# The last out-projection: token tiles in pairs, seven quarter products in place of eight

## The chip, the core and the metric

The kernel runs on one core of one Trainium2 chip. The metric is the device time of one execution in microseconds (us), the median over several runs. A core has TensorE (PE, matmuls; PEld is its loading of weights), VectorE (DVE), ScalarE (ACT), GpSimd (POOL) and SyncE (SP, which here only issues DMAs). Engines run their own queues in order and wait for each other by semaphores.

## The reference

A trunk of two layers over 2064 tokens (16 meta tokens and 2048 tokens) of 1024 channels. Layer 0 is a gated convolution module, layer 1 gated linear attention (GLA). After each layer comes a residual sum and a LayerNorm:

```python
for i in range(DEPTH):                       # DEPTH = 2
    if i % N_MIXERS == 0:
        y = conformer_mixer(h, ...)
    else:
        y = gla_mixer(h, ...)                # ends with (o * silu(r)) @ w_out
    h = layer_norm(DN_ALPHA * h + y, post_ln_g[i], post_ln_b[i])
return h[:, N_META:]
```

What the change touches is the end of layer 1 alone: `(o * silu(r)) @ w_out`, a product of 2048 x 1024 by 1024 x 1024, the sum with `DN_ALPHA * h`, the LayerNorm and the store of the output. All is float32.

## The kernel before

Four phases follow each other: the convolution layer's projections and taps (`phase1`), its norm, gate and out-projection (`phase2`), the GLA projections and chunks (`phase3`), and the last out-projection (`phase4`). A float32 product is made of three matmuls: each operand is split into a high part (a copy on ACT in the reduced type) and a low part (a subtraction on VectorE or GpSimd; `split`, L72 to 74), and `mm3` (L102 to 108) adds high times high, high times low and low times high into one PSUM bank, for each of eight blocks of 128 channels.

`phase4` (L825 to 869) first drives `phase3` to its end; the generator `gla` holds the last steps of the last head. Then the loop over 16 tiles of 128 tokens: `gated` loads a tile of gated outputs from `og_d` (L836) and splits it; `xt` gets the residual (L857); `out_tile` (L372 to 377) runs 24 matmuls for each half of 512 columns and adds the PSUM bank to `xt` (row sum, L377); `ln_stats` (L379 to 389) takes mean and variance with two instructions on VectorE, an aggregate, and a power on GpSimd (L388); four scale-and-shift instructions on VectorE (L862, L864) finish the tile, which is stored (L868; the last one in two halves, L866).

PSUM for these products is three banks in turn (`pjt`). The splits use three pairs of buffers in turn (`pair`). The weights of the out-projection stand in SBUF in high and low parts, loaded and split by `load_half` (L810 to 822) while the last heads run. The small tiles of `phase4` (`rowb`, `xt`) reuse tags of phase 3's pool `hp` (opened in `phase3_init`, L464), so they take over single buffers of it.

The program is written with a tile framework: it traces the instructions in the order of the code and, when the program is built, sets the order on every engine by a list scheduling over a simulated timeline (`schedule_with_timeline_sim=True`); of the instructions that are ready, that which stands earlier in the code goes first. So the splits of a later tile can lie between steps of an earlier one. A tile that takes over memory of a closed pool waits for the last use of what lay there (`reuse_waits="tile"`).

## Time and profile before

| what | value |
|---|---|
| median of 3 runs | 1761.71 us (1760.18 to 1763.15) |
| profiled execution, its own time | 1762.52 us |
| its span, first to last instruction | 1760.8 us |
| TensorE busy | 1703.8 us, 97% |
| VectorE busy | 1401.8 us, 80% |
| GpSimd busy | 940.5 us, 53% |
| ACT busy | 844.8 us, 48% |
| matmuls in the last out-projection | 768 |

Busy time is the sum of the instructions' own times. Matmuls overlap in a pipeline, so their listed duration is longer than the distance from one to the next; the distance of starts is what a matmul costs in a full stream. Times in the views are counted from the span's start. A view of an engine in order of time gives start, duration, the instruction and, in brackets, the idle time before it and what ended that. The profiled execution is one run; its own time, and not the median, is what its spans add up to.

### The profile page before, as it was taken

To read this page: it belongs to the slowest core of one execution; us is meant where nothing else is said; L and a number is where in the kernel's file an instruction comes from. 1 tells how busy PE (TensorE), PEld (TensorE's weight loads), DVE (VectorE), ACT (ScalarE), POOL (GpSimd) and SP (SyncE) were. 2 spreads that over 40 slices of the span, in tenths; PEclk is the share of its full clock that TensorE was granted. 3 is DMA by queue.
4 is the path that set the end of the run, shared out by engine and by line. 5 is a ranking of instruction groups with operands and counts; after the bars stand their busy time and mean duration, and the time that the engine had idled before them with its cause. 6 is when DMAs were issued, how large, how long until landed. Compare 5 with 4: busy or idle time off the path is not lost.

```text
span 1760.8 us, 29085 instructions
## 1 busy us (share of the span) xinstructions
PE 1703.8 (97%) x11715; PEld 1515.1 (86%) x11715; DVE 1401.8 (80%) x1893; ACT 844.8 (48%) x1293; POOL 940.5 (53%) x675
## 2 busy tenths in 40 slices
...
DMA packets 103911, 178.72 MB, mean 102 GB/s; under 512 B 8624, under 2 KB 68400, under 8 KB 103776
## 3 DMA queue, kind: packets, MB, share of 16 engines
...
q14 instruction: 43, 0.35, 0.1%
...
## 4 chain that ended last, share of the span: by engine, by line
PE 67%; DVE 17%; ACT 5%; POOL 4%; issue 4%; DMA 2%; SPq 0%; DVEq 0%; POOLq 0%; ACTq 0%
PE pj_y L107 4%; PE pj_y L108 4%; PE pj_y L106 4%; PE pj_g L107 3%; PE pj_g L106 3%; PE pj_g L108 3%; PE pj_z L107 3%; PE pj_a L107 3%; PE pj_z L106 3%; PE pj_a L106 3%; PE pj_z L108 3%; PE pj_a L108 3%; DVE A L712 2%; DVE A L711 2%; PE att L718 1%
## 5 line engine op out<-in xcount | busy, mean ns | idle before, releaser
L196 POOL TENSOR_TENSOR gacc<-gacc,prod 128x1024 f32<-128x1024 f32 (+1 forms) x156 | 386.3, 2479 | 64.6 <-ACT prod L195 55.7
L204 DVE SCALAR_TENSOR_TENSOR cacc<-glu,prm,cacc 128x1024 f32<-128x1024 f32 (+1 forms) x292 | 374.9, 1294 | 7.0
L708 POOL TENSOR_TENSOR A<-b 128x256 f32<-128x256 f32 x96 | 79.6, 829 | 305.1 <-PE att L718 119.1
L195 ACT ACTIVATE prod<-glu,prm 128x1024 f32<-128x1024 f32 (+1 forms) x156 | 179.3, 1156 | 108.4 <-POOL gacc L196 108.0
L106 PE MATMUL pj_g<-xh,h_w 128*128 128x412 f32 (+1 forms) x320 | 114.1, 357 | 6.0 <-ACT h_w L73 4.3
L107 PE MATMUL pj_g<-xl,h_w 128*128 128x412 f32 (+1 forms) x320 | 114.0, 356 | 0.3 <-DVE xl L74 0.3
L108 PE MATMUL pj_y<-woh,l_gt 128*128 128x512 f32 (+1 forms) x272 | 108.6, 405 | 5.2 <-DVE l_gt L74 5.1
L108 PE MATMUL pj_g<-xh,l_w 128*128 128x412 f32 (+1 forms) x320 | 112.7, 353 | 0.0
L107 PE MATMUL pj_a<-xl,h_w 128*128 128x412 f32 (+1 forms) x320 | 112.4, 351 | 0.0
L106 PE MATMUL pj_a<-xh,h_w 128*128 128x412 f32 (+1 forms) x320 | 112.3, 351 | 0.0
L107 PE MATMUL pj_z<-xl,h_w 128*128 128x412 f32 (+1 forms) x320 | 112.3, 351 | 0.0
L106 PE MATMUL pj_z<-xh,h_w 128*128 128x412 f32 (+1 forms) x320 | 112.2, 351 | 0.0
L108 PE MATMUL pj_z<-xh,l_w 128*128 128x412 f32 (+1 forms) x320 | 112.0, 351 | 0.0
L108 PE MATMUL pj_a<-xh,l_w 128*128 128x412 f32 (+1 forms) x320 | 111.9, 350 | 0.0
L106 PE MATMUL pj_y<-woh,h_gt 128*128 128x512 f32 (+1 forms) x272 | 110.4, 409 | 0.8 <-ACT h_gt L73 0.6
L107 PE MATMUL pj_y<-wol,h_gt 128*128 128x512 f32 (+1 forms) x272 | 110.3, 406 | 0.0
L106 PE MATMUL pj_y<-w4h,h_g 128*128 128x512 f32 x256 | 99.7, 390 | 0.0
L107 PE MATMUL pj_y<-w4l,h_g 128*128 128x512 f32 x256 | 99.6, 390 | 0.0
L108 PE MATMUL pj_y<-w4h,l_g 128*128 128x512 f32 x256 | 99.5, 389 | 0.0
L645 ACT ACTIVATE A<-A 128x512 f32<-128x512 f32 (+1 forms) x112 | 66.8, 598 | 55.1 <-POOL A L709 54.4
L388 POOL TENSOR_TENSOR rs<-rs,mhalf 128x1 f32<-128x1 f32 x16 | 14.5, 907 | 145.8 <-DVE rs L387 145.8
L377 DVE SCALAR_TENSOR_TENSOR xt<-xt,pj_y 128x512 f32<-128x512 f32 (+1 forms) x66 | 44.5, 678 | 59.2 <-PE pj_y L108 59.1
...
## 6 DMA issues: line engine op xcount, KB each, us to landing
r_w<-w SPq DMA_DIRECT2D x24, 512.0 KB, 3.2
c<-c_d SPq DMA_DIRECT2D x16, 512.0 KB, 4.6
szb<-sz_d SPq DMA_DIRECT2D x16, 512.0 KB, 4.5
xt<-x_tok SPq DMA_DIRECT2D x16, 512.0 KB, 4.6
h_d<-xt SPq DMA_DIRECT2D x16, 512.0 KB, 2.8
r_h1b<-h_d SPq DMA_DIRECT2D x16, 512.0 KB, 3.9
...
xt<-h_d SPq DMA_DIRECT2D x16, 512.0 KB, 3.5
```

The lines of the kernel that those rows point to most:

```text
L106: mm(out, lhsT=lh, rhs=rh, start=(i == 0), stop=False)
L107: mm(out, lhsT=lh, rhs=rl, start=False, stop=False)
L108: mm(out, lhsT=ll, rhs=rh, start=False, stop=(i == n - 1))
L195: nc.scalar.activation(pr, src(k), AF.Copy, scale=tap(k))
L196: nc.gpsimd.tensor_tensor(st["g"], st["g"], pr, op=ALU.add)
L204: nc.vector.scalar_tensor_tensor(out, src(k), tap(k), acc, op0=ALU.mult, op1=ALU.add)
L377: self.nc.vector.scalar_tensor_tensor(xt[:m, es], xt[:m, es], ALPHA, ps, op0=ALU.mult, op1=ALU.add)
L645: ex = lambda o, i: nc.scalar.activation(o, i, AF.Exp, scale=1.0 / TAU)
L708: nc.gpsimd.tensor_tensor(Av[:, :, 0], mid, bv[:, :, 0], op=ALU.subtract)
L711: nc.vector.tensor_tensor(Av[:, :, 0], Av[:, :, 0], kv[:, :, 0], op=ALU.mult)
L712: nc.vector.tensor_tensor(Av[:, :, 1], Av[:, :, 1], qv[:, :, 1], op=ALU.mult)
L718: nc.tensor.matmul(att[s : s + m, c, s + m : s + 2 * m], lhsT=A[:, a : a + m], rhs=A[:, a + m : a + 2 * m], start=False, stop=False, skip_ ...
```

## The change

Tiles 0 to 3 are computed as before. Tiles 4 to 15 go in six pairs. A pair is a block of 2 by 2 quarters: two tiles by two halves of the 1024 channels; the weight is 2 by 2 quarters as well. The pair's product is made of seven products of quarters (each 12 matmuls of 512 columns: four blocks of 128 channels, three matmuls each) in place of eight. For this,

- four sums of quarters of each pair are formed ahead (`forms`: two on VectorE, two on GpSimd) and split, with the two quarters of the first tile and one of the second;
- four sums of quarters of the weight are formed once (`weight_sums`, four calls during tiles 0 to 2, in the order 0, 3, 1, 2), from a second load of the weight, with subtractions on GpSimd and VectorE, and split;
- the products accumulate in three PSUM banks `x`, `y`, `z`: a bank is read after one product and the next product adds onto it (`add=True` in `mm3`). The first product goes through ACT to `s1` and is added to three of four quarters of the residual by GpSimd; the others are added by VectorE (`row_sum`, `add`);
- mean and variance of tiles 0 to 13 are taken by two passes on ACT with an accumulator; the last pair keeps `ln_stats`.

Residual tiles now hold a pair (two buffers), row vectors are whole rows, and all tiles of the phase lie in a new pool `p4`, opened after phase 3's pools `hp`, `c` and `gp` are closed. `weight_sums` stages its loads in the two buffers `junk`, which the ACT passes also use for their output.

```diff
--- before.py
+++ after.py
@@ -99,11 +99,11 @@
             out += [(h[:, k], l[:, k]) for k in range(nk)]
         return out
 
-    def mm3(self, out, ops):
-
-        mm, n = self.nc.tensor.matmul, len(ops)
+    def mm3(self, out, ops, add=False):
+
+        mm, n = partial(self.nc.tensor.matmul, skip_group_check=add), len(ops)
         for i, (lh, ll, rh, rl) in enumerate(ops):
-            mm(out, lhsT=lh, rhs=rh, start=(i == 0), stop=False)
+            mm(out, lhsT=lh, rhs=rh, start=(i == 0 and not add), stop=False)
             mm(out, lhsT=lh, rhs=rl, start=False, stop=False)
             mm(out, lhsT=ll, rhs=rh, start=False, stop=(i == n - 1))
 
@@ -461,8 +461,9 @@
         self.a1x = [c0.tile([P, P], F32, name=f"a1x{i}") for i in range(2)]
         for t in self.a1x:
             nc.gpsimd.memset(t, 0.0)
-        self.hp = self.pool(self.st3, name="p3h", bufs=2)
-        c = self.pool(self.st3, name="p3c", bufs=1)
+        self.st3l = ExitStack()
+        self.hp = self.pool(self.st3l, name="p3h", bufs=2)
+        c = self.pool(self.st3l, name="p3c", bufs=1)
         self.prm = c.tile([P, 8], F32, name="prm3")
         nc.sync.dma_start(self.prm[:, 0:6], pp)
         nc.vector.tensor_scalar(self.prm[:, 6:8], self.prm[:, 4:6], 0.5, None, op0=ALU.mult)
@@ -474,7 +475,7 @@
         nc.vector.tensor_tensor(self.wa2[64:96], raw[64:96], self.wa2[64:96], op=ALU.subtract)
         with ExitStack() as st:
             self.gla_consts(c, self.pool(st, name="p3k", bufs=1))
-        self.gp = self.pool(self.st3, name="p3g", bufs=2)
+        self.gp = self.pool(self.st3l, name="p3g", bufs=2)
         self.S = {}
 
     def block(self, bi):
@@ -819,12 +820,14 @@
             nc.sync.dma_start(r, wo[4 * e + k])
             self.split(r, h[:, k], l[:, k], nc.gpsimd if k == 1 else nc.vector)
             self.w4.append((h[:, k], l[:, k]))
+        self.w4t.append((h, l))
 
 
 
     def phase4(self, wo, rows, out):
         nc = self.nc
-        self.w4 = []
+        self.w4, self.w4t = [], []
+        self.uid = iter(range(1 << 20))
         gla = self.phase3(wo)
 
         last = (self.slot - 1) % len(self.slots)
@@ -845,27 +848,140 @@
             pass
         for _ in gla:
             pass
-        rb = []
-        for r, tags in enumerate((("gl", "ah"), "kq")):
-            rb.append([self.hp.tile([P, BMAX], F32, tag=t, name=f"rowb{r}{t}", bufs=1 + r)[:, :512] for t in tags])
+        self.st3l.close()
+        p4 = self.pool(self.st3, name="p4", bufs=1)
+        rb = [p4.tile([P, D], F32, name=f"rowb{r}") for r in range(2)]
+        for r in range(2):
+            nc.sync.dma_start(rb[r], rows[r : r + 1].broadcast_to([P, D]))
+        pairt = lambda nm, bufs=1: p4.tile([P, 2, D], F32, tag=nm, name=f"{nm}4_{next(self.uid)}", bufs=bufs)
+        half = lambda e: slice(512 * e, 512 * (e + 1))
+        last_pair = len(SUBS) // 2 - 1
+        add, sub = (partial(nc.vector.tensor_tensor, op=o) for o in (ALU.add, ALU.subtract))
+        gadd, gsub = (partial(nc.gpsimd.tensor_tensor, op=o) for o in (ALU.add, ALU.subtract))
+
+        def residual(p):
+            xt = pairt("xt", 2)
+            o = NMETA + 2 * P * p
+            nc.sync.dma_start(xt, self.h1_d[o : o + 2 * P].rearrange("(t p) d -> p t d", p=P))
+            return xt
+
+        def row_sum(ps, x):
+            nc.vector.scalar_tensor_tensor(x, x, ALPHA, ps, op0=ALU.mult, op1=ALU.add)
+
+        def norm_out(p, t, xt):
+            x, nm = xt[:, t], f"4{p}_{t}"
+            tk = slice(P * (2 * p + t), P * (2 * p + t + 1))
+            if p == last_pair:
+                rs = self.ln_stats(p4, x, P, nm)
+                mean, sub_mean = rs[:, 0:1], ALU.subtract
+            else:
+                rs = p4.tile([P, 4], F32, tag="rs4", name=f"rs{nm}", bufs=4)
+                junk = p4.tile([P, D], F32, tag="junk", name=f"junk{nm}", bufs=2)
+                nc.scalar.activation(junk, x, AF.Identity, accum_out=rs[:, 3:4])
+                nc.vector.tensor_scalar(rs[:, 0:1], rs[:, 3:4], -1.0 / D, None, op0=ALU.mult)
+                nc.scalar.activation(junk, x, AF.Square, bias=rs[:, 0:1], accum_out=rs[:, 1:2])
+                nc.vector.tensor_scalar(rs[:, 1:2], rs[:, 1:2], 1.0 / D, LN_EPS, op0=ALU.mult, op1=ALU.add)
+                nc.gpsimd.tensor_tensor(rs[:, 2:3], rs[:, 1:2], self.mhalf[:, 0:1], op=ALU.pow)
+                mean, sub_mean = rs[:, 0:1], ALU.add
             for e in range(2):
-                nc.sync.dma_start(rb[r][e], rows[r : r + 1, 512 * e : 512 * (e + 1)].broadcast_to([P, 512]))
-        for i in range(16):
-            tk = slice(P * i, P * (i + 1))
+                nc.vector.scalar_tensor_tensor(x[:, half(e)], x[:, half(e)], mean, rb[0][:, half(e)], op0=sub_mean, op1=ALU.mult)
+            for e in range(2):
+                nc.vector.scalar_tensor_tensor(x[:, half(e)], x[:, half(e)], rs[:, 2:3], rb[1][:, half(e)], op0=ALU.mult, op1=ALU.add)
+                if p == last_pair:
+                    nc.sync.dma_start(out[tk, half(e)], x[:, half(e)])
+            if p < last_pair:
+                nc.sync.dma_start(out[tk], x)
+
+
+
+        f12 = [p4.tile([P, 2, 4, 512], F32R, name=f"f12{x}") for x in "hl"]
+        f3 = [p4.tile([P, 4, 512], F32R, name=f"f3{x}") for x in "hl"]
+        f4 = [t[:, :, 512:] for t in self.w4t[0]]
+        w11, w21, w22 = ([x[:, :, half(e)] for x in self.w4t[k]] for k, e in ((0, 0), (1, 0), (1, 1)))
+        t4 = None
+
+        def weight_sums(k):
+            r1, r2 = (p4.tile([P, D], F32, tag="junk", name=f"ws{k}_{i}", bufs=2) for i in range(2))
+            nc.sync.dma_start(r1, wo[k])
+            nc.sync.dma_start(r2, wo[4 + k])
+            t12, t3 = (p4.tile([P, 2, 512], F32, tag=f"s{i}", name=f"t{i}_{k}") for i in (12, 34))
+            gsub(t12[:, 0], r1[:, half(1)], r1[:, half(0)])
+            sub(t3[:, 0], r2[:, half(1)], r1[:, half(1)])
+            gsub(t12[:, 1], r2[:, half(1)], t12[:, 0])
+            gsub(t4[k // 2][:, k % 2], r2[:, half(0)], t12[:, 1])
+            self.split(t12, f12[0][:, :, k], f12[1][:, :, k], nc.vector)
+            self.split(t3[:, 0], f3[0][:, k], f3[1][:, k], nc.vector)
+
+
+        t4 = [p4.tile([P, D], F32, tag=f"c{i}", name=f"t4{i}").rearrange("p (k c) -> p k c", k=2) for i in range(2)]
+        for i in range(4):
+            p, t = divmod(i, 2)
+            xt = xt if t else residual(p)
             h, l = gated(i, self.raw(f"c4{i}")[:, :D]) if i else g0
-            xt = self.hp.tile([P, 4, 256], F32, tag="vh" if i % 2 else "vl", name=f"xt4{i}").rearrange("p a b -> p (a b)")
-            nc.sync.dma_start(xt, self.h1_d[NMETA + P * i : NMETA + P * (i + 1)])
-            self.out_tile(h, l, self.w4, xt, P, f"y4{i}")
-            rs = self.ln_stats(self.gp, xt, P, f"4{i}")
-            halves = [slice(512 * e, 512 * (e + 1)) for e in range(2)]
-            for e, es in enumerate(halves):
-                nc.vector.scalar_tensor_tensor(xt[:, es], xt[:, es], rs[:, 0:1], rb[0][e], op0=ALU.subtract, op1=ALU.mult)
-            for e, es in enumerate(halves):
-                nc.vector.scalar_tensor_tensor(xt[:, es], xt[:, es], rs[:, 2:3], rb[1][e], op0=ALU.mult, op1=ALU.add)
-                if i == 15:
-                    nc.sync.dma_start(out[tk, es], xt[:, es])
-            if i < 15:
-                nc.sync.dma_start(out[tk], xt)
+            for e in range(2):
+                ps = self.pjt(f"y4{i}_{e}")
+                self.mm3(ps, [(h[:, k], l[:, k], self.w4[k][0][:, half(e)], self.w4[k][1][:, half(e)]) for k in range(KD)])
+                row_sum(ps, xt[:, t, half(e)])
+            if i < 3:
+                weight_sums(i)
+                if not i:
+                    weight_sums(3)
+            norm_out(p, t, xt)
+        for i in range(2):
+            self.split(t4[i], *(x[:, 2 * i : 2 * i + 2] for x in f4), nc.vector)
+
+        def forms(p):
+
+            c = []
+            for t in range(2):
+                r = self.raw(f"c4{p}_{t}")[:, :D] if p % 2 == 0 else p4.tile([P, D], F32, tag=f"c{t}", name=f"c4{p}_{t}")
+                o = P * (2 * p + t)
+                nc.sync.dma_start(r.rearrange("p (k n) -> p k n", n=P), self.og_d[:, :, o : o + P])
+                c.append(r.rearrange("p (a n) -> p a n", a=2))
+            (a11, a12), (a21, a22) = ((x[:, 0], x[:, 1]) for x in c)
+            s12, s34 = (p4.tile([P, 2, 512], F32, tag=f"s{i}", name=f"s{i}_{p}") for i in (12, 34))
+            two = lambda nm: [t[:, :D].rearrange("p (a n) -> p a n", a=2) for t in self.pair(nm)]
+            a1 = two(f"g4a{p}")
+            self.split(c[0], *a1, nc.vector)
+            add(s12[:, 0], a21, a22)
+            sub(s12[:, 1], s12[:, 0], a11)
+            b = two(f"g4b{p}")
+            self.split(s12, *b, nc.vector)
+            gsub(s34[:, 0], a11, a21)
+            gsub(s34[:, 1], a12, s12[:, 1])
+            d = two(f"g4c{p}")
+            self.split(s34, *d, nc.vector)
+            e = [p4.tile([P, 1, 512], F32R, tag=f"a22{x}", name=f"a22{x}_{p}") for x in "hl"]
+            self.split(a22, *(x[:, 0] for x in e), nc.vector)
+            q = lambda pr, i: [x[:, i].rearrange("p (k n) -> p k n", n=P) for x in pr]
+            return q(a1, 0), q(b, 1), q(a1, 1), q(d, 0), q(b, 0), q(e, 0), q(d, 1)
+
+        for p in range(2, last_pair + 1):
+            xt = residual(p)
+            fs = forms(p)
+            x, y, z = (self.pjt(f"y4{p}_{i}") for i in range(3))
+            prod = lambda ps, f, w, add: self.mm3(ps, [(f[0][:, k], f[1][:, k], w[0][:, k], w[1][:, k]) for k in range(4)], add)
+            f1, f2 = ([t[:, i] for t in f12] for i in range(2))
+            prod(x, fs[0], w11, False)
+            s1 = p4.tile([P, 512], F32, tag="p1", name=f"p1_{p}")
+            nc.scalar.activation(s1, x, AF.Copy, scale=1.0 / ALPHA)
+            gadd(xt[:, 0, half(1)], xt[:, 0, half(1)], s1)
+            x1 = xt[:, 1].rearrange("p (e c) -> p e c", e=2)
+            gadd(x1, x1, s1.unsqueeze(1).to_broadcast([P, 2, 512]))
+            prod(y, fs[1], f2, False)
+            row_sum(y, xt[:, 0, half(1)])
+            prod(x, fs[2], w21, True)
+            row_sum(x, xt[:, 0, half(0)])
+            prod(y, fs[3], f3, True)
+            row_sum(y, xt[:, 1, half(1)])
+            prod(z, fs[4], f1, False)
+            add(xt[:, 1, half(1)], xt[:, 1, half(1)], z)
+            prod(y, fs[5], f4, True)
+            row_sum(y, xt[:, 1, half(0)])
+            prod(z, fs[6], w22, True)
+            add(xt[:, 0, half(1)], xt[:, 0, half(1)], z)
+            norm_out(p, 1, xt)
+            norm_out(p, 0, xt)
         self.st3.close()
 
 
```

## Rows read from the trace of the kernel before

**Rows 1.** The busy table of the page: busy us, share of span, x instructions.

```profile
PE 1703.8 (97%) x11715; PEld 1515.1 (86%) x11715; DVE 1401.8 (80%) x1893; ACT 844.8 (48%) x1293; POOL 940.5 (53%) x675
```

**Rows 2.** Busy time by stage: length, busy by engine, granted clock, DMA share, GB/s.

```profile
core 0: us, PE busy (x) PEld busy (x) DVE busy (x) ACT busy (x) POOL busy (x), PEclk, DMA share, GB/s
...
1680.00:1700.00 20.00, 20.00 (x90) 16.57 (x89) 11.78 (x19) 2.13 (x2) 0.92 (x1) 1.00 0.47 155
...
1740.00:1761.00 21.00, 11.96 (x53) 9.57 (x51) 10.17 (x18) 0.00 (x0) 1.83 (x2) 0.87 0.13 51
```

**Rows 3.** Groups by line, 1400 to 1761: busy us, mean ns, idle before.

```profile
L106 PE MATMUL pj_y<-w4h,h_g 128*128 128x512 f32 x256 | 99.7, 390 | 0.0
```

**Rows 4.** VectorE in order of time, tiles 5 and 6: start, duration, instruction.

```profile
1643.20 0.69 DVE L377 SCALAR_TENSOR_TENSOR xt<-xt,pj_y 128x512 f32<-128x512 f32 x1 [4.02 <-PE pj_y L108]
1643.92 0.69 DVE L385 BATCH_NORM_STATS2 st<-xt 128x6 f32<-128x512 f32 x1
1644.53 1.21 DVE L74 TENSOR_TENSOR l_g<-r_c,h_g 128x1024 fp32r<-128x1024 f32 x1
1645.66 0.20 DVE L386 BATCH_NORM_AGGREGATE rs<-st 128x2 f32<-128x12 f32 x1
1645.89 0.15 DVE L387 TENSOR_SCALAR rs<-rs 128x1 f32<-128x1 f32 x1
...
1646.62 0.75 DVE L862 SCALAR_TENSOR_TENSOR xt<-xt,rs,rowb0ah 128x512 f32<-128x512 f32 x1
1647.29 0.75 DVE L864 SCALAR_TENSOR_TENSOR xt<-xt,rs,rowb1k 128x512 f32<-128x512 f32 x1
...
1654.08 0.69 DVE L377 SCALAR_TENSOR_TENSOR xt<-xt,pj_y 128x512 f32<-128x512 f32 x1 [4.02 <-PE pj_y L108]
```

**Rows 5.** Groups by line on ACT, 1540 to 1752.

```profile
L73 ACT ACTIVATE h_g<-r_c 128x1024 fp32r<-128x1024 f32 x15 | 15.9, 1063 | 115.0 <-PE pj_y L107 106.5 <-DMA r_c<-og_d 4.5 <-issue 4.0
...
L769 ACT ACTIVATION_READ_ACCUMULATOR kh<-o 128x1 f32 x8 | 1.6, 196 | 0.0
```

**Rows 6.** Groups by line and shape on GpSimd, whole span.

```profile
L423 POOL TENSOR_TENSOR xt<-xt,row 128x1024 f32<-128x1024 f32 x16 | 42.4, 2651 | 9.9 <-DVE xt L377 9.2 <-DVE rsl L331 0.7
...
L74 POOL TENSOR_TENSOR a_l<-at,a_h 128x512 fp32r<-128x512 f32 x16 | 24.5, 1534 | 81.7 <-ACT a_h L73 81.7
```

**Rows 7.** GpSimd in order of time, 1567 to 1575.

```profile
1567.93 0.61 POOL L708 TENSOR_TENSOR A<-b 128x256 f32<-128x256 f32 x1 [9.21 <-PE att L718]
...
1571.47 3.38 POOL L74 TENSOR_TENSOR w4l<-r_w,w4h 128x1024 fp32r<-128x1024 f32 x1
```

**Rows 8.** One line's instructions: duration ns min/median/max, first and last start.

```profile
L711 DVE TENSOR_TENSOR A<-A,b3k x24: 401/427/2618, 1411.6 to 1576.9; 128x256 f32<-128x256 f32 x24
```

**Rows 9.** VectorE in order of time, 1570 to 1576.

```profile
1570.96 1.63 DVE L74 TENSOR_TENSOR w4l<-w,w4h 128x1024 fp32r<-128x1024 f32 x1
1572.52 2.62 DVE L711 TENSOR_TENSOR A<-A,b3k 128x256 f32<-128x256 f32 x1
```

**Rows 10.** One line's instructions in the first stage (columns as in rows 8).

```profile
L204 DVE SCALAR_TENSOR_TENSOR cacc<-glu,prm,cacc x292: 1273/1290/1309, 57.5 to 541.1; 128x1024 f32<-128x1024 f32 x76, 128x1040 f32<-128x1040 f32 x70
L204 DVE SCALAR_TENSOR_TENSOR cacc<-glu,prm,gacc x16: 1301/3420/3512, 53.6 to 510.3; 128x1024 f32<-128x1024 f32 x8, 128x1040 f32<-128x1040 f32 x8
```

**Rows 11.** TensorE in order of time, the last transposes of phase 3.

```profile
1611.74 1.03 PE L780 MATMUL oT<-ident,osb 128*128 128x128 f32 x8
```

**Rows 12.** VectorE in order of time, 1614 to 1622.

```profile
1614.53 0.75 DVE L782 SCALAR_TENSOR_TENSOR og<-oT,prm,b3r 128x512 f32<-128x512 f32 x1
...
1621.44 0.69 DVE L377 SCALAR_TENSOR_TENSOR xt<-xt,pj_y 128x512 f32<-128x512 f32 x1 [3.51 <-PE pj_y L108]
```

**Rows 13.** DMA issues, 1540 to 1761: count, KB each, median us to landing.

```profile
w<-wo SPq DMA_DIRECT2D x2, 512.0 KB, 3.4
```

**Rows 14.** VectorE in order of time, the end of the kernel.

```profile
1752.00 0.69 DVE L377 SCALAR_TENSOR_TENSOR xt<-xt,pj_y 128x512 f32<-128x512 f32 x1 [4.02 <-PE pj_y L108]
...
1755.75 0.74 DVE L864 SCALAR_TENSOR_TENSOR xt<-xt,rs,rowb1q 128x512 f32<-128x512 f32 x1
```

## The prediction

> **What bounds the kernel now.** I read the busy table, then the table by stage of the end, then one tile of the last out-projection on VectorE. TensorE is busy for 97% of the span [rows 1]. In the last stage it never stops: 20.00 us of every 20 us up to 1740, at full clock, with VectorE near 11.8 us and GpSimd under 2 us [rows 2]. The stage is 16 tiles of 48 matmuls, 768 in three groups of 256 [rows 3]. Their listed 0.39 us is the length of one in a pipeline, not its price. The price comes from the row sums of the same half of two successive tiles, at 1643.20 and 1654.08: 10.88 us for 48 matmuls, 0.2267 us each [rows 4]. VectorE waits 4.02 us there for TensorE, so TensorE sets the pace. The order on each engine is fixed when the program is built, so an instruction that is late holds back all behind it on its engine.
>
> **What is removed.** A pair of tiles takes 96 matmuls, eight products of 12; seven take 84. Six pairs save 72 x 0.2267 = 16.3 us. All of it is TensorE time in a stage where TensorE is the bound, so it is the whole possible gain, 0.93%. A pair would take 84 x 0.2267 = 19.04 us, a product 2.72. The statistics on VectorE (two of 0.69 us, one of 0.20 and one of 0.15 a tile [rows 4]) leave it in 14 tiles; VectorE idles there now, so this gives nothing by itself.
>
> **VectorE and ACT in a pair.** By the distance of starts in [rows 4] a split of 1024 columns costs 1.13 us on VectorE, a scale-and-shift instruction of 512 columns 0.665, a row sum out of PSUM about 0.69. An add of 512 columns I estimate as half a split, 0.6. A pair has 3.5 splits (4.0), two adds (1.2), six reads of PSUM (4.1), eight scale-and-shift (5.3) and small ones (0.6): 15.2 us of the 19.04. ACT gets 3.5 copies of 1.06, one of 0.6, and four passes for the statistics of about 1.06 + 0.19 [rows 5]: near 9.5 us. Both fit. Loads and stores are the same bytes for the tiles; the DMA share stays near its 0.47 [rows 2].
>
> **GpSimd and VectorE take turns.** A pair adds on GpSimd three adds of 512 columns and one of 1024. The nearest rows are 1.53 us for 512 and 2.65 for 1024 [rows 6], taken beside a busy VectorE; from the free pass of 0.61 us for 256 columns [rows 7] I estimate 1.25 and 2.3: 6 us a pair, with the power of each tile a little more. In the last stage of before GpSimd has almost nothing, so the two are not seen together there; just before it they are. A multiply on VectorE whose median is 0.43 us [rows 8] took 2.62, from 1572.52 to 1575.06 [rows 9], while GpSimd ran one subtraction until 1574.85 [rows 7]. That subtraction, begun at 1571.47, took 3.38 us, and VectorE held a split until 1572.59 [rows 9]: each waited for a whole instruction of the other. In the first stage the same multiply-add on VectorE takes 1.29 us with one input in PSUM, and 3.42 in the median with both in SBUF [rows 10], while GpSimd is busy with long adds. So I price strict turns for VectorE instructions that read two SBUF tensors (splits, adds, scale-and-shift: 10.5 us a pair) and none for row sums out of PSUM. [...]
>
> **The stall inside a pair.** The third product adds onto x and the fourth onto y, in PSUM that must have been read first. The fourth may start only when the row sum after the second has read y; that row sum waits for GpSimd's add of s1, that for ACT's copy of x. TensorE reaches the fourth product 3 x 2.72 = 8.16 us after the pair's start. Until then VectorE has the end of the pair before, which stands earlier in the program: its last sum (until 0.8 us), four scale-and-shift of its second tile (2.7), the split of the last forms (1.13, not before the last product of the pair before has ended), four of its first tile (2.7, behind two ACT passes of 1.25 and a power). With no turns the row sum ends at 0.8 + 2.7 + 1.13 + 2.7 + 0.69 = 8.0 us, just in time. With the add of 512 in between it is 9.3, with that of 1024 too 11.6, with the waits for ACT and the power (estimated 1.5) 13.1. The stall is 0 (row sum ordered ahead of the scale-and-shift) to 4.9 us, in each of the five pairs that follow a pair; a gain is excluded, the saved products being counted already. I take 2.5, between the sums with one add and with both: 12.5 us; ends 0 and 24.5. All of TensorE's queue waits with it, since only matmuls of later pairs stand behind.
>
> **The change of stage.** The new pool lies where phase 3's working tiles lay, so its tiles wait until those are read for the last time. Adding up sizes in order of allocation (row vectors 8 KB, weight sums 32 and 16, t4 8, residuals 16, staging 8, sums 8), t3 falls on osb, read by the transposes of 1611.74 to 1612.8 [rows 11], and the low half of the first sums on parameters that og still reads at 1614.53 [rows 12]. Tile 4 starts at 1621.44, with the row sum of tile 3's last half [rows 12]. The four weight sums go through two staging buffers: a load of 3.4 us [rows 13], two subtractions of 1.25 that read the second buffer, 0.7 between steps: 6.6 us a round. Three rounds after 1613.5 end at 1633.3; the last split (1.06 on ACT, 1.13 on VectorE) at 1635.5. From 1621.4 TensorE can run the first and third product of pair 2 and half of the second, 6.8 us, to 1628.2: a wait of 7.3. It grows by some 3 us for each statistics pass that takes a staging buffer in between (ACT's passes of the first tiles use the same two): 13 to 15. If phase 3's tail comes 8 us earlier it is nil. I take 8, near the sum without such passes; ends 0 and 15. The second loading of the weights, 8 x 512 KB, costs nothing else: half of the DMA engines' time is free [rows 2].
>
> **The end.** Before, the last row sum starts at 1752.00 and VectorE ends at 1756.5 [rows 14]: 4.5 us. After, the other tile of the pair becomes ready only one product earlier: 4.3 us of work for it and 4.4 for the last, less 2.72: 6.0. It costs 1.5; bounds 0 and 4.
>
> **Sum.** -16.3 + 8 + 12.5 + 1.5 = +5.7 us. The profiled execution took 1762.5 (span 1760.8), so 1768.2; it stands 0.8 above the median of 1761.7, so I expect a median near 1768.
>
> **The rivals.** *Waits hidden, faster*: the row sum stands ahead of the scale-and-shift, or TensorE's fifth product, which needs no y, ahead of the fourth; and the last weight sum is there by 1628. It decides when the row sum starts within 7.5 us of the pair's start. With 1.5 at the end and some 5 of odd waits: -9.8, 1752. For it: 15.2 of 19.04 us on VectorE, and the order of before, in which the split of a later tile already lies between steps of an earlier one [rows 4]. Against it: the turns. *Even*: only one of the two waits, -16.3 + 1.5 + 12.5: -2.3, 1760. *Full turns*: every GpSimd add holds VectorE, 15.2 + 6 and 2 of gaps, 23.2 us a pair, 4.2 over, in six pairs 25; with 8 and 1.5: +18, 1780. [...] *It does not do what it says*: the code leaves no room for it; the count of matmuls would stay at 768.
>
> **How the numbers follow.** About 0.2% (3.5 us) is what a measurement of this kernel can tell from no change. Forecast 0.35 and full turns 0.15, both slower: 0.5. Waits hidden 0.33, faster. Even 0.17, same. The time is the forecast's, 1768; its own range is 1764 to 1776. With the cases of both signs the range is 1751 to 1783, which leaves about 1 in 10 on each side.
>
> **What the profile after would show.** 696 matmuls of 512 columns in the stage, 0.2267 us apart while they run. If I am right, TensorE idles between 1625 and 1645 behind weight sums; then each pair has a gap of 1 to 5 us ahead of the fourth product, ended by VectorE's row sum; scale-and-shift instructions beside GpSimd adds last over 1 us. If TensorE is busy 20 of 20 us from pair 2 on, the price of the turns is wrong; if it idles at another product, the place is wrong; if there is no gap before pair 2, the staging is.

## The result, and the profile after

The kernel after the change takes 1793.45 us in the median (1792.13 to 1798.15), the kernel before beside it 1761.66: a ratio of 1.0186, 95% interval 1.0174 to 1.0199. In the medians it is slower by 31.8 us. The profiled execution took 1798.15, the longest of the four and 4.7 above their median; its span is 1796.4, 35.6 above that of before. TensorE runs 11643 matmuls in place of 11715 [rows 1]: the 72 are gone, so the change does what it says.

The kernel after, busy time by stage of 20 us: start and end, length, busy (and count) of PE, PEld, DVE, ACT and POOL, granted clock of TensorE, DMA share, GB/s.

```profile
1600.00:1620.00 20.00, 8.35 (x25) 6.46 (x24) 7.32 (x9) 2.32 (x3) 4.64 (x4) 0.53 0.75 273
1620.00:1640.00 20.00, 20.00 (x89) 16.53 (x89) 15.43 (x17) 8.35 (x12) 10.54 (x7) 1.00 0.34 122
1640.00:1660.00 20.00, 13.01 (x50) 10.26 (x49) 20.00 (x23) 11.87 (x18) 13.86 (x9) 0.83 0.69 210
1660.00:1680.00 20.00, 16.81 (x66) 12.96 (x65) 15.37 (x19) 3.24 (x4) 6.95 (x6) 0.91 0.36 133
1680.00:1700.00 20.00, 20.00 (x87) 16.05 (x86) 18.05 (x26) 9.42 (x14) 8.02 (x5) 1.00 0.38 126
1700.00:1720.00 20.00, 17.85 (x76) 13.92 (x75) 16.46 (x23) 7.79 (x12) 9.59 (x6) 1.00 0.39 137
1720.00:1740.00 20.00, 17.55 (x77) 13.91 (x75) 17.03 (x24) 8.86 (x13) 8.60 (x6) 1.00 0.38 130
...
1760.00:1780.00 20.00, 15.96 (x67) 12.33 (x66) 12.83 (x22) 6.26 (x10) 5.53 (x4) 0.98 0.28 105
```

Where [rows 2] had TensorE at 20.00 of every 20 us, there are now three kinds of holes: one of 12 us at the start (1600 to 1620), one of 10 us at the change from tiles to pairs (1640 to 1680), and one of 1 to 4 us in most stages of the pairs (20.00 less the first figure of a line).

The first hole. The kernel after, SyncE's queue in order of time: start, duration, what was issued.

```profile
1601.80 0.98 SPq L787 DMA_DIRECT2D og_d<-og  x2
1602.84 0.94 SPq L855 DMA_DIRECT2D rowb<-rows  x2
1603.83 0.43 SPq L865 DMA_DIRECT2D xt<-h_d  x1
1604.30 0.47 SPq L905 DMA_DIRECT2D ws<-wo  x1
```

VectorE in the same kernel, in brackets the idle time before an instruction and what ended it:

```profile
1612.11 1.88 DVE L869 SCALAR_TENSOR_TENSOR xt<-xt,pj_y 128x512 f32<-128x512 f32 x3 [6.75 <-DMA xt<-h_d]
...
1650.44 0.67 DVE L869 SCALAR_TENSOR_TENSOR xt<-xt,pj_y 128x512 f32<-128x512 f32 x1
```

Every load of the new pool stands behind the last store of `og` in SyncE's queue. The residual of tiles 0 and 1 is issued at 1603.83 and is there at 1612.11, 8.3 us later, beside the row vectors and 1 MB of weights. Until then no row sum can empty a PSUM bank, and TensorE, with three banks full, stops for 11.65 us, up to 1612.85. Whether the order of the queue alone held these loads back, or also buffers of phase 3 under the new pool, no run separates. TensorE's first matmul behind tile 3 starts at 1642.96, in the kernel before at 1621.24: 21.7 us late. The row sum of tile 3's last half, at 1621.44 in [rows 12], comes at 1650.44, another 7 us later, as VectorE has steps of the weight sums and of earlier tiles ahead of it.

The kernel after, TensorE's waits between 1590 and 1800: who waited for whom, us in total, times, the longest.

```profile
PE pj_y L106 <- DVE xt L869: 20.1, 5, 11.6
PE pj_y L106 <- ACT p L967: 7.0, 1, 7.0
...
PE pj_y L108 <- DVE l_g4a L74: 2.9, 1, 2.9
```

The second hole. The kernel after, SyncE's loads for the weight sums in order of time.

```profile
1615.43 0.33 SPq L905 DMA_DIRECT2D ws<-wo  x1
1618.21 0.33 SPq L906 DMA_DIRECT2D ws<-wo  x1
1626.38 0.33 SPq L905 DMA_DIRECT2D ws<-wo  x1
1629.41 0.33 SPq L906 DMA_DIRECT2D ws<-wo  x1
...
1636.60 0.33 SPq L905 DMA_DIRECT2D ws<-wo  x1
```

ACT, the end of a statistics pass that writes to a staging buffer:

```profile
1629.20 0.19 ACT L882 ACTIVATION_READ_ACCUMULATOR junk<-xt,rs 128x1 f32 x1
```

GpSimd in the round that begins at 1615.43:

```profile
1622.76 1.89 POOL L910 TENSOR_TENSOR t<-ws,t 128x512 f32<-128x512 f32 x1 [1.61 <-DMA ws<-wo]
1624.73 1.63 POOL L911 TENSOR_TENSOR t<-ws,t 128x512 f32<-128x512 f32 x1
```

A round takes 10.2 to 11.1 us (the first load of all is that of 1604.30, above): two loads one behind the other, then subtractions, here of 1.89 and 1.63 us. Each load waits until its staging buffer has been read for the last time. The second load of this round waits for GpSimd, which reads that buffer twice; those of the two rounds after it, at 1629.41 and 1640.35, wait for ACT's statistics passes, 5.9 us in all. The fourth round starts at 1636.60, and its last split ends near 1650. ACT's copy of the first product stands behind these splits and two more passes of statistics in ACT's queue and lets TensorE go at 1652.84.

The third kind, one pair. The kernel after, VectorE in order of time.

```profile
1702.36 0.69 DVE L869 SCALAR_TENSOR_TENSOR xt<-xt,pj_y 128x512 f32<-128x512 f32 x1 [2.23 <-DMA xt<-h_d]
1703.03 0.68 DVE L982 TENSOR_TENSOR xt<-xt,pj_y 128x512 f32<-128x512 f32 x1
...
1704.83 4.53 DVE L887 SCALAR_TENSOR_TENSOR xt<-xt,rs,rowb 128x512 f32<-128x512 f32 x2
...
1711.40 1.40 DVE L887 SCALAR_TENSOR_TENSOR xt<-xt,rs,rowb 128x512 f32<-128x512 f32 x2
...
1717.11 0.68 DVE L869 SCALAR_TENSOR_TENSOR xt<-xt,pj_y 128x512 f32<-128x512 f32 x1
```

GpSimd beside it:

```profile
1702.40 1.29 POOL L968 TENSOR_TENSOR xt<-xt,p 128x512 f32<-128x512 f32 x1 [10.09 <-DMA xt<-h_d]
1703.64 3.47 POOL L970 TENSOR_TENSOR xt<-xt,p 128x1024 f32<-128x1024 f32 x1
1707.06 1.75 POOL L950 TENSOR_TENSOR s<-c,c 128x512 f32<-128x512 f32 x1
```

And TensorE:

```profile
1717.84 0.50 PE L106 MATMUL pj_y<-w4h,a22h 128*128 128x512 f32 x1 [1.95 <-DVE xt L869]
```

Two things are to be seen. A row sum waits 2.23 us for the residual of its pair, and the last sum of the pair before (L982) stands behind it in VectorE's queue. Then two scale-and-shift instructions, which take 1.40 us together at 1711.40, take 4.53 beside GpSimd's add of 3.47 and the subtraction behind it. The row sum that empties bank y comes at 1717.11, and TensorE waits for it with the sixth product (its operand is `a22h`), not with the fourth. Over the six pairs such waits come to 6.7 us at the sixth product and 3.1 at the fourth.

The last matmul starts at 1786.22, 10.2 us ahead of the span's end; before it was 9.2. So the 35.6 us of this execution are: 22 at the start, 29 lost between tile 3 and the last matmul (143.5 us for 504 matmuls worth 114.3), 1 at the end, and the 16.3 saved.

### The profile page after: what moved, and what is told of

It reads as the page before. It is cut to its first block, busy times and chain, and to the rows that moved or that the text cites. A ratio compares the mean times of both kernels' runs of the same rounds, so it can differ in the third digit from the quotient of the medians.

```text
span 1796.4 us, 29142 instructions
## 1 busy us (share of the span) xinstructions
PE 1703.3 (95%) x11643; PEld 1509.9 (84%) x11643; DVE 1443.8 (80%) x1915; ACT 897.3 (50%) x1377; POOL 1004.2 (56%) x711
## 4 chain that ended last, share of the span: by engine, by line
PE 59%; DVE 20%; ACT 6%; issue 5%; POOL 5%; DMA 4%; SPq 0%; DVEq 0%; POOLq 0%; ACTq 0%
PE pj_g L107 3%; PE pj_g L106 3%; PE pj_g L108 3%; PE pj_z L107 3%; PE pj_a L106 3%; PE pj_z L106 3%; PE pj_a L107 3%; PE pj_z L108 3%; PE pj_a L108 3%; DVE A L713 2%; DVE A L712 2%; PE att L719 1%; PE pj_y L106 1%; PE pj_y L107 1%; PE pj_y L108 1%
## 5 line engine op out<-in xcount | busy, mean ns | idle before, releaser
L709 POOL TENSOR_TENSOR A<-b 128x256 f32<-128x256 f32 x96 | 79.9, 832 | 305.4 <-DVE b L635 124.7
L710 POOL TENSOR_TENSOR A<-b 128x256 f32<-128x256 f32 x96 | 81.7, 851 | 0.0
L74 POOL TENSOR_TENSOR a_l<-at,a_h 128x512 fp32r<-128x512 f32 x16 | 24.2, 1512 | 81.1 <-ACT a_h L73 81.1
L74 POOL TENSOR_TENSOR l_w<-r_w,h_w 128x1024 fp32r<-128x1024 f32 x24 | 60.5, 2521 | 13.9 <-ACT h_w L73 13.9
L106 PEld LDWEIGHTS pj_g<-xh,h_w 128*128 128x128 f32 x320 | 61.1, 191 | 8.0 <-ACT h_w L73 4.2
L108 PEld LDWEIGHTS pj_y<-woh,l_gt 128*128 128x128 f32 (+1 forms) x272 | 50.7, 186 | 20.0 <-DVE l_gt L74 6.9
```

Source lines behind the costliest of these rows:

```text
L74: eng.tensor_tensor(lo, raw, hi, op=ALU.subtract)
L106: mm(out, lhsT=lh, rhs=rh, start=(i == 0 and not add), stop=False)
L108: mm(out, lhsT=ll, rhs=rh, start=False, stop=(i == n - 1))
L709: nc.gpsimd.tensor_tensor(Av[:, :, 0], mid, bv[:, :, 0], op=ALU.subtract)
L710: nc.gpsimd.tensor_tensor(Av[:, :, 1], bv[:, :, 1], mid, op=ALU.subtract)
```

## The experiments

Eighteen kernels, each timed in turns with the kernel before, whose median was 1760.3 to 1762.0 in these series. The "distance of pairs" below is worked out from the split of the last forms (`l_g4c`) on VectorE: its start in the last of six pairs less that in the second, by four. In the kernel after it is 21.48 us (1686.09 to 1771.99); ideal would be 19.04.

**The start.** All sixteen tiles plain, in the new pool, weight sums formed and not used:

```diff
-        for i in range(4):
+        for i in range(16):
...
-        for p in range(2, last_pair + 1):
+        for p in ():
```

> The twelve tiles of the pairs are computed as plain tiles (two halves of 24 matmuls) in the new pool, with the statistics on ACT; the weight sums are formed but not used, and the second split of t4 is left out. Theory A (the first loads of the new pool stand behind the tail of phase 3, 21 us, whatever comes later): 1783, with the first row sum of the stage near 1612 and tile 4 starting near 1643. Rival (the pairs alone cost the time, the pool only its own few us): 1760 to 1766, tile 4 near 1621.

1779.49, ratio 1.0101 (1.0084 to 1.0117). No pair is left, and it is slower by 18 us. Its first row sum on VectorE:

```profile
1609.14 1.88 DVE L869 SCALAR_TENSOR_TENSOR xt<-xt,pj_y 128x512 f32<-128x512 f32 x3 [9.07 <-DMA xt<-h_d]
```

From 1620 on TensorE is at 20.00 of 20. So the late start costs 18 by itself, and the six pairs another 14 where 16 was to be saved.

The start undone: `hp` stays open, row vectors and residuals (tile by tile) lie in its small buffers as before, and some small tiles with them.

```diff
-        self.hp = self.pool(self.st3l, name="p3h", bufs=2)
+        self.hp = self.pool(self.st3, name="p3h", bufs=2)
...
-            xt = pairt("xt", 2)
+            xt = [self.hp.tile([P, 4, 256], F32, tag=g, ...) for g in ("vh", "vl")]
```

> Phase 3's pool hp stays open and holds row vectors and residuals in its small tags as in the kernel before (residuals in tiles of 512 KB, two pairs), and some small tiles; the rest of the new pool is smaller. Theory A: the first row sum comes near 1581 and tile 4 starts near 1621; if all of the 21 us is kept, 1773. If the four weight sums, which still start after phase 3's tail, then hold up pair 2 (rival: given back later), 1780 to 1790, with TensorE idle between 1628 and 1645.

1791.72, ratio 1.0172 (1.0157 to 1.0187): only 1.7 better. TensorE is full until 1620 and then idle for 31 of 40 us. What was won at the start is given back ahead of the first pair.

**The adds.** GpSimd's three adds of the first product left out:

```diff
-            gadd(xt[:, 0, half(1)], xt[:, 0, half(1)], s1)
-            x1 = xt[:, 1].rearrange("p (e c) -> p e c", e=2)
-            gadd(x1, x1, s1.unsqueeze(1).to_broadcast([P, 2, 512]))
```

> The two adds of s1 on GpSimd are left out (three of four quarters lack the first product). Theory of turns as forecast: row sum and scale-and-shift no longer wait for GpSimd, 2.5 to 4 us a pair, time 1775 to 1781. Theory B: the loop loses only what the adds took from its scale-and-shift, about 1 to 2 us a pair: 1784 to 1789, with row sums still ended by the residual's load.

1779.07, ratio 1.0103 (1.0088 to 1.0118): 14.4 better, 2.4 a pair. Pairs are 19.09 us apart, and TensorE is full from 1660 to 1760.

A third residual buffer, for which the operands lost their second:

```diff
-            xt = pairt("xt", 2)
+            xt = pairt("xt", 3)
...
-                r = self.raw(f"c4{p}_{t}")[:, :D] if p % 2 == 0 else p4.tile([P, D], F32, tag=f"c{t}", name=f"c4{p}_{t}")
+                r = self.raw(f"c4{p}_{t}")[:, :D]
```

> Three residual buffers in place of two; the third takes the place of the two tiles that hold t4 and the odd pairs' operands. Theory B (the pair's period of 21.4 to 25 us is the loop output store, residual load, row sum, scale-and-shift, store over two buffers): the period falls to 19.0 to 20.5, the time by 6 to 12 us, to 1782 to 1788. Rival (turns of VectorE and GpSimd set the period): the period stays at 21.5, 1791 to 1796.

1800.24, ratio 1.0226 (1.0208 to 1.0244): worse, pairs 24.13 apart. No row sum waits for a residual, but now loads of the single operand buffer come late (GpSimd has idled 9.53 us when one ends its wait at 1680.64); it settles nothing on the residuals.

**The three causes together.** Early start, no weight sums (quarters of the weights in their place), no adds:

```diff
-            if i < 3:
-                weight_sums(i)
...
-            f1, f2 = ([t[:, i] for t in f12] for i in range(2))
...
+            f1, f2, f3 = ks(w11), ks(w21), ks(w22)
```

> The pairs with three things taken out: the late start (row vectors and residuals of the first tiles lie in phase 3's small buffers again), the weight sums (quarters of the weights stand in for them, so no second loading, no staging), and GpSimd's three adds of the first product. Part of the computation is changed by the last two. If these three hold the whole loss: 16.3 us saved, the longer end (4.6 in the profile of the changed kernel) paid, pairs 19.5 us apart as without the adds: 1761.5 - 16.3 + 4.6 + 2.5 = 1752 (1748 to 1755), with TensorE at 20 of 20 us from 1600 to 1750. Rival: the planner's interleaving of the products or the in-order VectorE holds TensorE up on its own account: 1758 or more.

1749.01, ratio 0.9936 (0.992 to 0.9953). The 4.6 of the expectation for the end was a misreading; by the last matmuls it is 1.0. Its first two stages from 1600 on:

```profile
1600.00:1620.00 20.00, 20.00 (x97) 16.76 (x96) 11.94 (x22) 7.89 (x15) 4.55 (x4) 1.00 0.60 178
1620.00:1640.00 20.00, 17.35 (x76) 14.00 (x76) 19.48 (x30) 7.23 (x11) 6.36 (x5) 1.00 0.56 166
```

-16.3, 1.0 at the end and the 2.7 + 0.8 us that TensorE still waits make -11.8; measured are -11.3. Pairs are 19.03 apart. Seven products cost TensorE what was forecast, the interleaving of products costs nothing, and the three causes hold the whole loss, to within half a us. To divide it, each was put in and out alone. Weight sums alone left out of the change:

```diff
-            if i < 3:
-                weight_sums(i)
...
-            f1, f2 = ([t[:, i] for t in f12] for i in range(2))
+            f1, f2, f3 = w11, w21, w22
```

> The changed kernel with the weight sums left out alone (quarters of the weights stand in for them, so part of the computation is changed; the same room is kept in the pool), late start and GpSimd's adds as in the change. If the late start and the weight sums are two costs, one behind the other: the wait of some 10 us ahead of the first pair goes, the late start of 18 stays: 1783 (1780 to 1786). If they overlap, so that the sums are hidden behind the late start: 1790 or more.

1784.88, ratio 1.0133 (1.0118 to 1.0148): 8.6 better, which looks like two costs in a row; but then the early start alone would have given 18 and not 1.7. Early start without adds, with the sums:

```diff
-        self.hp = self.pool(self.st3l, name="p3h", bufs=2)
+        self.hp = self.pool(self.st3, name="p3h", bufs=2)
...
-            gadd(xt[:, 0, half(1)], xt[:, 0, half(1)], s1)
...
-            gadd(x1, x1, s1.unsqueeze(1).to_broadcast([P, 2, 512]))
```

> Early start and GpSimd's adds left out (three quarters lack the first product), weight sums as in the change. Against the kernel that leaves the sums out too (1749) it prices the sums alone, against the one with the late start (1779) the start alone. If the sums, whose subtractions read buffers of phase 3's tail and go through one staging pair, come no earlier than with the late start: 1779 (1775 to 1785), the sums alone 30. If the early start carries through: 1765 or less.

1788.22, ratio 1.0152 (1.0137 to 1.0167): 9 slower than with the late start, and 3 above the range that was expected. SyncE's queue in this kernel:

```profile
1611.14 0.98 SPq L787 DMA_DIRECT2D og_d<-og  x2
1612.17 0.45 SPq L912 DMA_DIRECT2D ws<-wo  x1
...
1639.69 0.33 SPq L913 DMA_DIRECT2D ws<-wo  x1
```

ACT in the same kernel:

```profile
1645.05 0.63 ACT L73 ACTIVATE f3hb<-t 128x512 fp32r<-128x512 f32 x1 [5.38 <-DVE t L916]
...
1646.62 1.04 ACT L73 ACTIVATE f12h<-t 128x1024 fp32r<-128x1024 f32 x1
1647.57 0.57 ACT L975 ACTIVATE p<-pj_y 128x512 f32<-128x512 f32 x1
```

Its longest wait of TensorE:

```profile
PE pj_y L106 <- ACT p L975: 25.6, 1, 25.6
```

The chain of sums starts behind the last store of `og` here too, and that store now comes 9.3 us later (1611.14 for 1601.80), because TensorE runs six halves of plain tiles ahead of phase 3's tail and not three. So the chain ends later, and ACT's copy of the first product stands behind its splits in ACT's queue: TensorE waits 25.6 us in one piece. A copy of 0.57 us waits although its input has long been there: the last matmul of the first product starts at 1622.18, and the copy comes at 1647.57, although ACT stands idle for 5.38 us ahead of 1645.05.

Late start alone:

```diff
-            if i < 3:
-                weight_sums(i)
...
-            f1, f2 = ([t[:, i] for t in f12] for i in range(2))
+            f1, f2, f3 = w11, w21, w22
...
-            gadd(xt[:, 0, half(1)], xt[:, 0, half(1)], s1)
...
-            gadd(x1, x1, s1.unsqueeze(1).to_broadcast([P, 2, 512]))
```

> Late start alone: weight sums and GpSimd's adds both left out of the changed kernel (quarters of the weights stand in for the sums, three quarters lack the first product). Against 1749 with none of the three. If the late start is a wait at one place, 18 us as with sixteen plain tiles: 1767 (1764 to 1770). If it also upsets what follows (residuals of a pair in one load, two buffers): 1775 or more.

1767.78, ratio 1.0034 (1.0021 to 1.0048): a wait at one place, as with plain tiles; pairs 19.13 apart. Adds alone:

```diff
-        self.hp = self.pool(self.st3l, name="p3h", bufs=2)
+        self.hp = self.pool(self.st3, name="p3h", bufs=2)
...
-            if i < 3:
-                weight_sums(i)
...
-            f1, f2 = ([t[:, i] for t in f12] for i in range(2))
...
+            f1, f2, f3 = ks(w11), ks(w21), ks(w22)
```

> GpSimd's adds alone: early start, no weight sums, the adds in. Against 1749 with none of the three. If the adds cost the 1 to 2.4 us a pair by which the pairs with adds stood further apart than those without (20 to 21.5 against 19.1), from the first of six pairs on: 1758 (1755 to 1763). If they cost only where residuals come late, in the changed kernel: 1751 or less.

1761.16, ratio 0.9998 (0.9988 to 1.0007): 12 above the kernel with none of the three, 3 more than the middle of what was expected. By the second pair 9.6 of it are there (the split of its last forms starts at 1656.61, in that kernel at 1646.97); from there on pairs are 19.83 apart.

| late start | weight sums | adds on GpSimd | median us |
|---|---|---|---|
| no | no | no | 1749.0 |
| yes | no | no | 1767.8 |
| no | yes | no | 1788.2 |
| no | no | yes | 1761.2 |
| yes | yes | no | 1779.1 |
| yes | no | yes | 1784.9 |
| no | yes | yes | 1791.7 |
| yes | yes | yes | 1793.5 |

Put in alone, the three cost 18.8, 39.2 and 12.2: 70 us. Together they cost 44.5. Taken out of the change alone they give 1.7 (start), 8.6 (sums) and 14.4 (adds). The late start and the sums hide behind each other, since both count from the same store. The adds cost 3.5 to 17.1 us, depending on which of the other two is there. A "no" under late start stands for the whole group of that edit: row vectors, residuals loaded tile by tile, and small tiles in phase 3's buffers.

**What the adds cost.** First by VectorE out of PSUM, no copy on ACT and no add on GpSimd:

```diff
-            nc.scalar.activation(s1, x, AF.Copy, scale=1.0 / ALPHA)
-            gadd(xt[:, 0, half(1)], xt[:, 0, half(1)], s1)
...
+            row_sum(x, xt[:, 0, half(1)])
+            for e in range(2):
+                row_sum(x, xt[:, 1, half(e)])
```

> The changed kernel, but the first product is added to its three other quarters by VectorE straight out of PSUM (three row sums of 512 columns of about 0.69 us, 2.1 us a pair more on VectorE), not by ACT's copy and GpSimd's adds. Complete computation. If turns between GpSimd and VectorE set the 21 to 25 us of a pair: they go, a PSUM read takes no turn, VectorE has some 17.3 us a pair, under 19.04; pairs 19 to 20 us apart, about 1779, as with the adds left out (ratio 1.008 to 1.012). Rival: the amount of work on the in-order VectorE, and not the turns: 17.3 us and its gaps are then as long as before, pairs stay at 21 us or more: 1788 or more.

1801.33, ratio 1.0231 (1.0215 to 1.0246). Against the expectation it is slower than the change: pairs 22.18 apart. VectorE is not full (14.7 to 16.6 of 20); it waits for residuals, and TensorE for it. Then with a third residual buffer, the staging of the weight sums; ACT's passes get a buffer of their own, so that the staging is free of them too, and the total holds both changes:

```diff
-            xt = pairt("xt", 2)
+            xt = pairt("x3") if p in (4, 7) else pairt("xt", 2)
...
-                junk = p4.tile([P, D], F32, tag="junk", name=f"junk{nm}", bufs=2)
+                junk = p4.tile([P, D], mybir.dt.bfloat16, tag="junk", name=f"junk{nm}", bufs=1)
```

> First product added by VectorE out of PSUM, and besides a third buffer for the residuals of a pair: the 8 KB in which the weight sums are staged, free by then; ACT's statistics write their throw-away output to 2 KB of their own. Operands keep both buffers. Complete computation. If pairs are held by a loop (store of the output, load of the next residual into the buffer, row sum of the first product that waits for it at the head of VectorE's queue, statistics and scale-and-shift of the pair before behind it): no row sum in the pairs ends with a wait for the residual, pairs 19 to 20 us apart, 1778 to 1784. Rival: the length of VectorE's own queue in a pair sets the distance, loads or not: 21 us or more, 1790 or more.

1784.85, ratio 1.0132 (1.0115 to 1.0149), pairs 20.39. VectorE's row sums of the first product, in the kernel with two buffers:

```profile
1704.90 0.69 DVE L869 SCALAR_TENSOR_TENSOR xt<-xt,pj_y 128x512 f32<-128x512 f32 x1 [1.45 <-DMA xt<-h_d]
```

And in that with three:

```profile
1705.21 1.87 DVE L869 SCALAR_TENSOR_TENSOR xt<-xt,pj_y 128x512 f32<-128x512 f32 x3
```

In the pairs (from 1660 on) row sums wait 6.4 us for residuals with two buffers and nothing with three. So with the adds out of PSUM a loop sets the distance: store of a pair, load of the next residual into its buffer, the row sum that waits for it at the head of VectorE's queue, and behind that the steps that lead to the next store. With three buffers (and ACT's own buffer) and the adds on GpSimd as in the change:

```diff
-            xt = pairt("xt", 2)
+            xt = pairt("x3") if p in (4, 7) else pairt("xt", 2)
```

> The changed kernel with the same third residual buffer and both operand buffers, the adds of the first product on GpSimd as in the change. Complete computation. If turns cost by themselves: no wait for residuals, yet pairs at 21 us or more, scale-and-shift beside GpSimd's adds over 1 us, about 1788 (1785 to 1793), some 8 above the kernel with the same buffers and the adds out of PSUM. If the loop through the residual buffers is all: pairs at 19 to 20 us, 1778 to 1784, no different from that kernel.

1790.97, ratio 1.0165 (1.015 to 1.0181), pairs 21.83: no row sum in the pairs waits for a residual any more (7.5 us in the change), and yet they come no closer while GpSimd adds (what the kernel gains, it gains ahead of the second pair, where the staging is also free of ACT's passes; the split of that pair's last forms starts at 1676.44 there and at 1686.09 in the change). The same adds on VectorE:

```diff
-            gadd(xt[:, 0, half(1)], xt[:, 0, half(1)], s1)
+            add(xt[:, 0, half(1)], xt[:, 0, half(1)], s1)
```

> The kernel with three residual buffers and ACT's copy of the first product, its adds on VectorE from SBUF and not on GpSimd: same operations, same dependencies, only the engine is another. Complete computation. If the turns with GpSimd are what its adds cost: VectorE has 1.9 us more of its own a pair but waits for no add; pairs at 20.4 us as with the adds out of PSUM, 1785 (1782 to 1788). If GpSimd's adds cost nothing by their turns: VectorE is only longer, 1791 or more, as with the adds on GpSimd.

1786.71, ratio 1.0149 (1.0132 to 1.0166), pairs 20.49. The intervals of the totals overlap; in the traces the pairs differ. One pair of each on VectorE in order of time, first with the adds on GpSimd:

```profile
1698.20 1.22 DVE L74 TENSOR_TENSOR l_g4c<-s,h_g4c 128x1024 fp32r<-128x1024 f32 x1
...
1706.59 3.55 DVE L889 SCALAR_TENSOR_TENSOR xt<-xt,rs,rowb 128x512 f32<-128x512 f32 x2
...
1719.97 1.22 DVE L74 TENSOR_TENSOR l_g4c<-s,h_g4c 128x1024 fp32r<-128x1024 f32 x1
```

Then with the adds on VectorE:

```profile
1721.50 1.22 DVE L74 TENSOR_TENSOR l_g4c<-s,h_g4c 128x1024 fp32r<-128x1024 f32 x1
...
1728.75 0.68 DVE L969 TENSOR_TENSOR xt<-xt,p 128x512 f32<-128x512 f32 x1
1729.35 1.21 DVE L971 TENSOR_TENSOR xt<-xt,p 128x1024 f32<-128x1024 f32 x1
...
1742.31 1.22 DVE L74 TENSOR_TENSOR l_g4c<-s,h_g4c 128x1024 fp32r<-128x1024 f32 x1
```

21.77 against 20.81 in these two, 21.83 against 20.49 over four pairs: the adds cost 1.0 to 1.3 us a pair more on GpSimd, although VectorE itself works 1.9 longer without it. Two scale-and-shift instructions, 1.40 us elsewhere, take 3.55 beside GpSimd's add of 2.85 (begun at 1706.08): a turn; but an add also lasts longer on GpSimd (1.43 at 1704.69 for 0.68), and a row sum waits for it. What each of the two is worth, no run separates. On VectorE the adds still leave the pairs 1.4 further apart than without them (19.09).

**More cover for the sums.** Adds out of PSUM and the early start:

```diff
-        self.hp = self.pool(self.st3l, name="p3h", bufs=2)
+        self.hp = self.pool(self.st3, name="p3h", bufs=2)
...
-            gadd(xt[:, 0, half(1)], xt[:, 0, half(1)], s1)
...
+            row_sum(x, xt[0][:, half(1)])
```

> As the kernel before this one (first product added out of PSUM), with the early start: row vectors and first residuals in phase 3's small buffers. If the start that is won is given back ahead of the first pair, where the weight sums come no earlier, as it was with the adds on GpSimd: 1.5 to 3 below the kernel before this one, about 1777 (1774 to 1780), TensorE idle some 30 us between 1620 and 1660. Rival: the two gains add up (18 less): 1761 or below.

1790.1, ratio 1.0164 (1.0149 to 1.0179): 11.2 below the kernel with adds out of PSUM and two pair buffers (1801.33), but above what was expected, as that kernel had been expected at 1779. TensorE waits 30.9 us in one piece ahead of the first pair. The same with eight plain tiles and four pairs:

```diff
-        for i in range(4):
+        for i in range(8):
...
-        for p in range(2, last_pair + 1):
+        for p in range(4, last_pair + 1):
```

> As the kernel before this one, with eight plain tiles ahead and four pairs, so that the weight sums have 43.5 us more of TensorE's work to hide behind. If the wait ahead of the first pair is only the weight sums coming late (up to 31 us of idle time), it is gone: 4 x 2.72 = 10.9 us saved, 4.6 paid at the end, 4 x 0.46 for pairs of 19.5: about 1757 (1754 to 1760), ratio 0.997, TensorE at 20 of 20 from 1600 to 1740. Rival: the weight sums hold up the plain tiles too (VectorE full, GpSimd's subtractions taking turns with it) and the wait only moves: 1765 or more.

1771.93, ratio 1.0063 (1.0046 to 1.008): the wait is spread, not gone. That with the sums spread over tiles 0, 2, 4 and 5 and their staging shared with nothing:

```diff
-            if i < 3:
-                weight_sums(i)
-                if not i:
-                    weight_sums(3)
+            if i in (0, 2, 4, 5):
+                weight_sums((0, 9, 3, 9, 1, 2)[i])
```

> Eight plain tiles, four pairs, the early start, the first product added out of PSUM, and now the four weight sums spread over tiles 0, 2, 4 and 5, with a staging buffer that ACT's statistics do not write to. If the 12 us that TensorE still lost between 1620 and 1690 with eight plain tiles came from weight sums crowding VectorE's and GpSimd's queues beside tiles 0 to 2 and from the shared staging: 1760 (1757 to 1764). Rival: the pairs' own loop and the residual buffers take the time, wherever the sums stand: 1768 or more.

1768.58, ratio 1.004 (1.0025 to 1.0055), at the rival's 1768 or more. VectorE is busy 19.56 of 20 us between 1620 and 1640, and TensorE waits 5.3 there. On it a third residual buffer:

```diff
-            xt = [self.hp.tile([P, 4, 256], F32, tag=g, ...) for g in ("vh", "vl")]
+            xt = [pairt("x3")] if p == 6 else [self.hp.tile([P, 4, 256], F32, tag=g, ...) for g in ("vh", "vl")]
```

> The kernel with eight plain tiles, early start and spread weight sums (1768.6), with the staging of the sums as a third residual buffer for the seventh pair of tiles. Complete computation. In that kernel the pairs still stood 20 to 22 us apart and VectorE waited for residuals 6 us. If the residual loop is what is left in the pairs: 3 to 5 less, 1764. If VectorE's order is, with or without the loads: no change, 1768.6.

1768.04, ratio 1.0033 (1.0019 to 1.0048): no change. On that, all of GpSimd's adds and subtractions of this stage on VectorE:

```diff
-        gadd, gsub = (partial(nc.gpsimd.tensor_tensor, op=o) for o in (ALU.add, ALU.subtract))
+        gadd, gsub = (partial(nc.vector.tensor_tensor, op=o) for o in (ALU.add, ALU.subtract))
```

> The kernel before this one with all of GpSimd's subtractions (12 in the weight sums, two a pair) on VectorE, so that no long GpSimd operation is left in the stage. Complete computation. VectorE gets 12 x 0.7 + 8 x 0.7 = 14 us more of its own, but in the plain tiles' stretch its scale-and-shift instructions lose the 1 us that each lasted longer beside a subtraction. If turns make VectorE the bound between 1620 and 1660 (19.6 busy of 20 us, 5.3 us wait of TensorE): 1760 (1757 to 1763). If its own work does: 1770 or more.

1768.67, ratio 1.0042 (1.0027 to 1.0057): again no change. The wait went from one place to another, as two of its stages show:

```profile
1620.00:1640.00 20.00, 19.42 (x86) 15.78 (x85) 19.94 (x32) 8.07 (x12) 2.95 (x3) 1.00 0.71 230
...
1660.00:1680.00 20.00, 13.26 (x45) 9.49 (x44) 19.71 (x33) 12.32 (x18) 1.54 (x2) 0.74 0.70 220
```

TensorE is nearly full beside the plain tiles now, and loses 6.7 us at the first pair, where the granted clock is 0.74 in the mean, with VectorE at 19.71 of 20. No complete version came out below the kernel before.

## Why the prediction was right or wrong

The direction was right, the size not: 1768 foretold, 1793.45 measured, above the range's end of 1783.

- **The saving**, -16.3: right. 72 matmuls fewer, pairs 19.03 us apart where nothing holds them up.
- **VectorE and ACT fit into a pair**: right. With the adds left out TensorE stays full.
- **The stall inside a pair**, 12.5 in all: with the adds taken out of the change, 14.4 go, 2.4 a pair for 2.5. That the size fits is partly luck, as the same adds cost 3.5 to 17.1 us in the table. The cause was right in part. With three residual buffers, where no row sum waits for a residual, GpSimd's adds cost 1.0 to 1.3 us a pair more than the same adds on VectorE, by turns or by their own length. Another 1.4 the adds cost on VectorE as well; that this is VectorE's longer queue is argued and not shown. That the residual's load waits for the store of two pairs earlier was not in the working: with the adds out of PSUM it is worth 1.8 a pair (22.18 to 20.39), with the adds on GpSimd nothing (21.48 and 21.83). The place was wrong too: the planner lets products of two pairs alternate, and the wait falls on the sixth product more than on the fourth. What the residuals cost beside GpSimd's adds stays open: with residuals loaded tile by tile pairs were 19.98 apart, with three pair buffers 21.83, and these kernels differ in more than the loads.
- **The change of stage**, 8 with ends 0 and 15: the step that failed. Late start and sums together cost 30.1 (1779.1 less 1749.0). First, that the row vectors and residuals of the first tiles move into the new pool was seen, as sizes and addresses, but their loads were priced at nothing. They stand behind the store of `og` in SyncE's queue, and the residual's 8.3 us had no cover. Alone that is 18.8. Second, the sums were priced too low. The case of the working, pair 2 ready near 1620 and the sums behind the last store, is the early start without adds: there TensorE waits 25.6 us and not 7.3. The chain of sums reaches ACT's last copy of them at 1646.6 to 1647.7 there, where the last split was to end at 1635.5; and the working let the third product and half of the second run meanwhile, but the copy of the first product, which the third needs, stands behind the sums in ACT's queue. In the change a round was 10.2 to 11.1 us, not 6.6: loads that wait for a staging buffer, subtractions of 1.5 to 1.9 and not 1.25, and, in two rounds, the statistics passes in the same buffers, which the working named (13 to 15 with them) and left out of its 8. Third, the escape that was named, that phase 3's tail comes 8 us earlier, did happen (the last store of `og` at 1601.80), and it was no gain: with three banks full TensorE had no plain tile left to run ahead of that tail.
- **The end**, 1.5: measured 1.0.
- **The sum** again, with these values: -16.3 + 30.1 + 14.4 + 1.0 + 3.5 (odd waits, in the kernel with none of the three) = 32.7; measured 31.8. The 30.1 and 14.4 are differences between measured kernels, so only the other terms are put to the test by it.
- **The rivals.** "Waits hidden" (1752) is the kernel with none of the three causes, 1749; in the change its condition failed, as the last weight sum was there near 1650 and not by 1628. "Even" (1760) fell, as both waits came. "Full turns" (1780) is nearer to the measured time than the forecast, but not by its cause: pairs stood 21.48 apart and not 23.2. "It does not do what it says" fell with the 72 matmuls. Of the signs that were to show the forecast wrong, one came, a wait at another product. No gap before pair 2, or none in the pairs, did not come; the gap before it, 1640 to 1670, came 15 us later than foretold, by the late start.
